# Mixed attention and expert layer, one core: expert weights in 2 MB pieces with 16 KB rows to a partition

## The chip, the core and the metric

One core of one Trainium2 chip runs the whole program. The metric is the device time of one execution in microseconds (us); less is better. All data is in the chip's main memory (HBM) at the start, and the result is written back there.

## The reference, cut to what matters

One transformer-like layer on 256 latent tokens of 1024 channels, with 256 context tokens. A first part (attention, a gated linear attention and an output projection) makes `x_next`. The second part is a mixture of 32 experts, and it is the part that the change is about:

```python
h2 = rms_norm(x_next, norm2) * (1 + sc2) + sh2
logits = h2 @ w_router + b_router               # top 4 of 32 experts for each token
...
gu   = xb @ w1[e] + b1[e]                       # w1: 1024 x 2048 fp32 for each expert, 8 MB
gate = minimum(gu[:, :1024], 7.0)
up   = clip(gu[:, 1024:], -7.0, 7.0)
act  = gate * sigmoid(1.702 * gate) * (up + 1)
y    = act @ w2[e] + b2[e]                      # w2: 1024 x 1024 fp32 for each expert, 4 MB
...
x = x_next + gt2 * weighted_sum_of_the_four(y)
```

Everything is fp32. The weights of all experts are 32 x 12 MB = 402.65 million bytes, and the kernel reads each of them once.

## The kernel before

The kernel is written with a framework that places the tiles, sets the waits and chooses the order of the instructions on each engine by a schedule of its own; the order on an engine is then fixed. All transfers between HBM and the on-chip memory (SBUF) are issued by SyncE (SP in the profile), one after another: an issue that waits for its buffer holds up all issues behind it. The bytes of a transfer are spread over 16 DMA engines, 8 of the 128 partitions to each.

**The first part** (up to about 325 us) loads its weights by `raw_load` (L115) into a pool `wp` of four rotating buffers of 8 KB to a partition. `split` (L120) makes of each fp32 piece a high and a low part (ScalarE L123, VectorE L124) in a second pool `spl` of two buffers, also of 8 KB. The last weights that go this way are the four pieces of `w_out` (L871). Their output is `xn`, from which `hsc`, `h2h` and `h2l` are made (L894 to L897): the normalised tokens, and their high and low parts. Router, top 4 and positions follow (L901 to L928), then a gather by matmul (`gather`, L1000) that puts the tokens of an expert into columns of `xs`, at most 63 of them; the rest, if any expert has more, goes to a fallback loop (L1180) that does not run here.

**The expert part.** For expert e, `layer1` (L1027) multiplies `xs` with the eight blocks of 128 rows of w1 (k = 0 to 7), each block in one 1 MB piece with a row of 8 KB to a partition. `scale1` (L1034) copies the two PSUM banks to `gu` on ScalarE (L1038); `fold` (L1041) transposes and adds the two halves by matmul (L1044), adds the bias `b1T` and does the activation (L1047 to L1055) into `x.a`. `layer2` (L1057) multiplies `x.a` with w2, four 1 MB pieces of two blocks of 128 rows, two rows of 4 KB to a partition. `scatter` (L1072) adds the result to the output banks. The order is layer 1 of expert e, then layer 2 of expert e-1; the list `order` (L949) has the loads in the same order: 8 pieces of w1, then 4 of w2, 384 pieces in all.

**The buffers of the pieces** (`load_next`, L958) are taken in turn from 15 places of 1 MB: four of a pool `raw2`, the two halves of `xhl`, the four buffers of `wp`, the two halves of `xhh`, the two of `spl` and one of `mp`. `raw2` and `xhl` come free early. Those of `wp` and `spl` come free when the pieces of `w_out` have been split and used, one after another; `xhh` (the memory of `yh`, `yl`) after the last matmul of `w_out` (L797); that of `mp` after the router. `weights` (L987) hands a piece to the matmuls.

Other names in the rows: `ml`, `wb`, `wo` are weights of the first part, `wb` and `wo` with rows of 2 KB; `c` is the bank of layer 2, `g` that of layer 1, `t` that of fold, `ga` or `y` that of gather, `y` also the output.

Of the kernel before, what the change touches and what calls it, by code (L numbers as in the profile page):

```python
# [73 lines left out]
def layer(tc, t, dbg=None):  # L74
# [10 lines left out]
    dram = es.enter_context(tc.tile_pool(name="dram", bufs=1, space=DRAM))  # L85
    wp = es.enter_context(tc.tile_pool(name="wp", bufs=2))
    spl = es.enter_context(tc.tile_pool(name="spl", bufs=2))

# [3 lines left out]
    hhf = hh.rearrange("p k n -> p (k n)")  # L92
    NRAW, NMORE, NSPL = 4, 1, 2

# [20 lines left out]
    def raw_load(src, name):  # L115
        r = wp.tile(list(src.shape), F32, tag="raw", name=name, bufs=NRAW)
        queue.append(sp.dma_start(r, src))
        return r

    def split(r, name, after=None):  # L120
        hl_ = spl.tile([P, 2] + list(r.shape[1:]), F32R, tag="w", name=name + "s", bufs=NSPL)
        h, l = hl_[:, 0], hl_[:, 1]
        a = act.activation(h, r, AF.Copy)  # L123
        b = dve.tensor_sub(l, r, h.bitcast(F32))  # L124
        if after:
            behind(a, after[0])
            behind(b, after[1])
        return h, l
# [95 lines left out]
    load_mod(1)  # L224
    load_pa(1)
    queue.append(sp.dma_start(wlr, win[:, 2304:2336].rearrange("(k p) n -> p k n", p=P)))
    pbch = kchunks(win, 512, 512, "pb")
    for a, b in zip(queue, queue[1:]):
        behind(b, a)
    front = queue[-1]  # L230

# [246 lines left out]
    clr = bx.tile([P, 33 * P], F32R, tag="lsg", name="clr")  # L478
    clu = wp.tile([P, 33 * P], U8, tag="raw", name="clu", bufs=NRAW)
    sp.dma_start(clu, t["cl"])  # L480
# [347 lines left out]
    sp.dma_start(rt[0:16], mrow[:, D:3 * D].rearrange("o (k p) -> (o k) p", p=P))  # L828
    sp.dma_start(rt[16:24], t["norm2"].rearrange("o (k p) -> (o k) p", p=P))
    wr = mx.tile([P, KB, NE], F32, name="wr")  # L830
    sp.dma_start(wr, t["w_router"][0].rearrange("(k p) n -> p k n", p=P))
    brb = keep.tile([P, NE], F32, name="brb")
    sp.dma_start(brb, t["b_router"].to_broadcast([P, NE]))
    b1T = keep.tile([P, NE, 16], F32, name="b1T")
    bt = mx.tile([P, 4, P], F32, name="bt")
    sp.dma_start(bt, t["b_exp_in"][0].rearrange("e (b p) -> (e b) p", p=P).rearrange("(j p) n -> p j n", p=P))
    b1p = glb("b1p")
    for j in range(4):
        pe.transpose(b1p[:, j * P:(j + 1) * P], bt[:, j], ident)
    dve.tensor_copy(b1T, b1p.rearrange("p (e b) -> p e b", b=16))  # L840
    rtp = glb("rtp")
# [28 lines left out]
    for n in range(2):  # L870
# [76 lines left out]


    order = []  # L949
    for e in range(NE + 1):  # L950
        if e < NE:
            order += [(e, k) for k in range(KB)]
        if e:
            order += [(e - 1, KB + q) for q in range(KB // 2)]
    loads, ready = [0], {}
    NROT = 4 + 2 * NRAW + NSPL + NMORE

    def load_next():  # L958
        n = loads[0]
        loads[0] += 1  # L960
        if n >= len(order):
            return
        e, k = order[n]
        m = n % NROT
        if m < NRAW:
            r = raw2.tile([P, 2048], F32, tag="raw", name=f"x{e}_{k}", bufs=NRAW)
        elif m < 2 + NRAW:
            m -= NRAW
            r = xhl[:, m * 2048:(m + 1) * 2048]
        elif m < 2 + 2 * NRAW:  # L970
            r = wp.tile([P, 2048], F32, tag="raw", name=f"x{e}_{k}", bufs=NRAW)
        elif m < 4 + 2 * NRAW:
            m -= 2 + 2 * NRAW
            r = xhh[:, m * 2048:(m + 1) * 2048]
        elif m < 4 + 2 * NRAW + NSPL:
            r = spl.tile([P, 2048], F32, tag="w", name=f"x{e}_{k}", bufs=NSPL)
        else:
            r = mp.tile([P, 2048], F32, tag="raw", name=f"x{e}_{k}", bufs=NMORE)
        if k < KB:
            sp.dma_start(r, w1[e][k * P:(k + 1) * P])  # L980
        else:
            q = k - KB
            sp.dma_start(r.rearrange("p (k n) -> p k n", k=2),
                         w2[e][q * 2 * P:(q + 1) * 2 * P].rearrange("(k p) n -> p k n", p=P))
        ready[e, k] = r

    def weights(e, k):  # L987
        while (e, k) not in ready:
# [38 lines left out]
    def layer1(x, xs, k):  # L1027
        w = weights(x.e, k)
# [28 lines left out]
    def layer2(x):  # L1057
        b = bank(gp, "c", f"c{x.e}")
        for q in range(KB // 2):
            w = weights(x.e, KB + q).rearrange("p (k n) -> p k n", k=2)  # L1060
            for kk in range(2):
                k = 2 * q + kk
                for n in range(2):
                    pe.matmul(b[n * CAP:(n + 1) * CAP], x.a[:, k], w[:, kk, n * 512:(n + 1) * 512],  # L1064
                              start=k == 0, stop=k == KB - 1)
        oh = mp.tile([P, 512], F32R, tag="oh", name=f"oh{x.e}", bufs=2)
# [113 lines left out]
    with tc.If(most > LIM):  # L1180
# [18 lines left out]
        with tc.For_i(0, NE, 1) as e:  # L1199
# [80 lines left out]
```

## Time and profile before

| | us |
|---|---|
| runs shown | 1317.69, 1317.51, 1295.82 (median 1317.51) |
| the profiled execution | 1295.6 |
| its span, first to last instruction | 1293.8 |

TensorE (PE) is busy 1202.9 us of the span, VectorE (DVE) 383.5, ScalarE (ACT) 254.9, GpSimd (POOL) 45.3. In the chain that ended last PE has 55% and DMA 39%. Busy PE is not PE at its peak: matmuls are pipelined and their ends are modelled. "PEld" is the weight load of PE. A row of the timeline has the start in us, the duration, the engine, the line, what is written from what, the number of instructions merged, and in brackets the idle time before it with what ended it.

### The profile page before, as it was taken

What the parts mean: (1) busy time and instruction counts of PE and PEld (TensorE: products, weight loads), DVE (VectorE), ACT (ScalarE), POOL (GpSimd) and SP (SyncE); (2) the same over time, 40 slices, a digit from 0 to 9 for tenths busy, and PEclk for the clock granted to TensorE, in tenths of its full rate; (3) what the DMA queues carried; (4) which work ended last, traced back from release to release, by engine and by line L of the source; (5) the groups of instructions that cost most, each with busy time, mean ns of one, the idle gap of its engine ahead of it and who ended that gap; (6) DMA issues with size and microseconds to landing.
All of it is one profiled execution on the core that took longest, in us unless ns stands there. A gap on an engine that the chain in (4) does not pass through costs nothing.

```text
span 1293.8 us, 14788 instructions
## 1 busy us (share of the span) xinstructions
PE 1202.9 (93%) x6050; PEld 564.5 (44%) x6050; DVE 383.5 (30%) x830; ACT 254.9 (20%) x445; POOL 45.3 (3%) x52
## 2 busy tenths in 40 slices
PE   6999999999899999999989998999899899988886
PEld 4667868767443344333323332333333333322222
DVE  4556766457411131311111111211121111111113
ACT  3453433434111111111111111111111111111110
POOL 1201000002200000000000000000000000000000
PEclk9999999999899999999999999999999999999998
DMA  9856111895999999999999999999999999999995
GB/s 344 295 174 229 67 48 54 320 385 183 352 414 418 417 417 417 417 418 417 417 417 417 416 417 417 416 417 419 417 417 417 418 419 417 416 416 417 417 417 213
DMA packets 98707, 463.80 MB, mean 358 GB/s; under 512 B 10270, under 2 KB 12418, under 8 KB 63818
## 3 DMA queue, kind: packets, MB, share of 16 engines
q1 hardware_dynamic: 98636, 462.82, 89.4%
q8 instruction: 49, 0.80, 0.3%
q14 instruction: 22, 0.18, 0.0%
HBM read 461.73 MB, written 1.06 MB: 358 GB/s over the span
## 4 chain that ended last, share of the span: by engine, by line
PE 55%; DMA 39%; DVE 2%; issue 1%; ACT 1%; POOL 1%; SPq 0%; POOLq 0%; DVEq 0%; ACTq 0%
DMA x<-in_w_exp_in 32%; PE g L1031 14%; PE c L1064 12%; DMA x<-in_w_exp_out 5%; PE t L1044 4%; PE pg L289 3%; PE br L797 2%; PE pa L289 2%; DMA xhh<-in_w_exp_out 2%; PE pc L289 1%; PE pb L289 1%; PE ml L395 1%; PE o L697 1%; PE e L535 1%; PE a L560 1%
## 5 line engine op out<-in xcount | busy, mean ns | idle before, releaser
L1031 PE MATMUL g<-x,xs 128*64 128x512 f32 x1536 | 365.5, 600 | 35.9 <-DMA x<-in_w_exp_in 35.9
L1031 PEld LDWEIGHTS g<-x,xs 128*64 128x64 f32 x1536 | 100.7, 136 | 261.9 <-issue 153.7
L1047 DVE TENSOR_TENSOR o<-t,b1T 128x512 f32<-128x512 f32 x64 | 44.3, 692 | 543.5 <-PE t L1044 543.5
L1064 PE MATMUL c<-x,a 128*64 128x512 f32 x720 | 172.5, 603 | 0.6 <-DMA x<-in_w_exp_out 0.6
L1038 ACT ACTIVATE gu<-g,ws 128x512 f32<-128x512 f32 x64 | 43.6, 687 | 456.2 <-PE g L1031 455.2
L1044 PEld LDWEIGHTS t<-cf,gu 128*128 128x128 f32 x512 | 62.0, 191 | 51.2 <-ACT sg L1052 22.7
L1064 PEld LDWEIGHTS c<-x,a 128*64 128x64 f32 x720 | 44.7, 136 | 68.9 <-issue 56.3
L1044 PE MATMUL t<-cf,gu 128*128 128x128 f32 x512 | 74.0, 288 | 0.0
L1031 PE MATMUL g<-xhl,xs 128*64 128x512 f32 x256 | 63.0, 600 | 5.4 <-DMA xhl<-in_w_exp_in 5.4
L1031 PE MATMUL g<-xhh,xs 128*64 128x512 f32 x256 | 62.1, 599 | 5.4 <-DMA xhh<-in_w_exp_in 5.4
L1052 ACT ACTIVATE sg<-o 128x256 f32<-128x256 f32 x64 | 26.6, 416 | 158.2 <-DVE o L1050 158.2
L1069 DVE SCALAR_TENSOR_TENSOR ol<-c,ws,oh 128x512 fp32r<-128x512 f32 x32 | 24.0, 749 | 82.8 <-ACT oh L1068 82.8
L1068 ACT ACTIVATE oh<-c,ws 128x512 fp32r<-128x512 f32 x32 | 22.0, 688 | 109.8 <-PE c L1064 109.8
L1064 PE MATMUL c<-xhl,a 128*64 128x512 f32 x160 | 39.6, 605 | 0.6 <-DMA xhl<-in_w_exp_out 0.6
L1007 DVE COPY xs<-ga 128x252 f32<-128x252 f32 x28 | 11.8, 421 | 87.8 <-PE ga L1003 87.8
L1031 PEld LDWEIGHTS g<-xhh,xs 128*64 128x64 f32 x256 | 17.3, 136 | 43.8 <-issue 27.1
L1031 PEld LDWEIGHTS g<-xhl,xs 128*64 128x64 f32 x256 | 17.5, 136 | 43.2 <-issue 27.2
L1003 PEld LDWEIGHTS ga<-G,h2h 128*128 128x128 f32 x112 | 16.7, 188 | 44.9 <-issue 44.9
L1064 PE MATMUL c<-xhh,a 128*64 128x512 f32 x144 | 34.6, 604 | 0.0
L1077 PE MATMUL y<-oh,st 64*128 64x512 f32 x128 | 23.7, 445 | 10.8 <-ACT oh L1068 8.7
L1054 DVE TENSOR_TENSOR sg<-sg,o 128x256 f32<-128x256 f32 x64 | 27.2, 425 | 17.9 <-ACT sg L1052 17.9
L1003 PE MATMUL ga<-G,h2h 128*128 128x256 f32 x112 | 28.2, 333 | 0.0
(583 smaller groups left out, 1336.7 us busy)
## 6 DMA issues: line engine op xcount, KB each, us to landing
x<-in_w_exp_in SPq DMA_DIRECT2D x192, 1024.0 KB
x<-in_w_exp_out SPq DMA_DIRECT2D x90, 1024.0 KB
xhl<-in_w_exp_in SPq DMA_DIRECT2D x32, 1024.0 KB
xhh<-in_w_exp_in SPq DMA_DIRECT2D x32, 1024.0 KB
xhl<-in_w_exp_out SPq DMA_DIRECT2D x20, 1024.0 KB
xhh<-in_w_exp_out SPq DMA_DIRECT2D x18, 1024.0 KB
ml<-in_w_mod SPq DMA_DIRECT2D x16, 1024.0 KB
wm<-in_w_mod SPq DMA_DIRECT2D x16, 512.0 KB
```

The lines of the kernel that those rows point to most:

```text
L289: m_ = pe.matmul(b[:, 0:m], a[:, k, i * P:(i + 1) * P], w[:, kk, 0:m], start=k == 0 and x == 0, stop=k == KB - 1 and x == 2)
L797: pe.matmul(b, a[:, k, i * P:(i + 1) * P], w[:, kk], start=first and p + kk + x == 0, stop=last and p == 1 and kk == 1 and x == 2)
L1003: pe.matmul(b[:, 0:256], src[:, i, k * P:(k + 1) * P], G[:, i, :, 0], start=hf + i == 0, stop=hf + i == 2)
L1031: pe.matmul(x.gu[h][u * CAP:(u + 1) * CAP], xs[:, x.e % GS, k], w[:, u * D + h * 512:u * D + h * 512 + 512], start=k == 0, stop=k == KB - 1)
L1038: act.activation(gu, x.gu[h], AF.Copy, scale=x.r)
L1044: pe.matmul(b[:, j * P:(j + 1) * P], x.gs[h][:, j * P:(j + 1) * P], foldm, start=True, stop=True)
L1047: dve.tensor_tensor(o, b.rearrange("p (b u s) -> p b u s", b=4, u=2), bias.unsqueeze(3).to_broadcast([P, 4, 2, CAP]), op=ALU.add)
L1052: act.activation(s, g, AF.Sigmoid, scale=1.702)
L1054: dve.tensor_mul(s, s, g)
L1064: pe.matmul(b[n * CAP:(n + 1) * CAP], x.a[:, k], w[:, kk, n * 512:(n + 1) * 512], start=k == 0, stop=k == KB - 1)
L1069: dve.scalar_tensor_tensor(ol, b, x.w, oh.bitcast(F32), op0=ALU.mult, op1=ALU.subtract)
L1077: pe.matmul(ys[i][n], x.st[r, i * P:(i + 1) * P], x.o[q][r], start=False, stop=x.e == NE - 1 and q == 1, skip_group_check=True)
```

## The change

Expert weights are loaded in pieces of 2 MB in which a partition has 16 KB of neighbouring rows: partition p of a w1 piece has rows 2p and 2p+1 of a block of 256, of a w2 piece rows 4p to 4p+3 of a block of 512. The tokens and the hidden units are permuted to match (`h2h`, `h2l`, `gu`, `b1T`, `shc`), so that the same products are summed. The 15 places of 1 MB become 7 of 2 MB, taken in turn, and one of 1 MB used once; one piece of expert 1 and the very last one are loaded in two halves of 1 MB. For this `wp` and `spl` are no longer pools with rotating buffers: `wp` is two fixed tiles of 16 KB to a partition, used in the first part as four places in turn by `raw_tile`, and `spl` is one tile with two halves. As a place is now given in the order of the program text, the calls of `load_pa(1)`, `wlr` and `pb` are moved down behind the code that reads the place before; the order of the queue is the same.

```diff
-    NRAW, NMORE, NSPL = 4, 1, 2
+    NRAW, NSPL = 4, 2
+    wpt = [wp.tile([P, 4096], F32, name=f"wpt{j}") for j in range(2)]
+    spt = spl.tile([P, 4096], F32R, tag="spt", name="spt")
+    ring = [0, 0]
+
+    def raw_tile(shape, name=None, dt=F32):
+        n = ring[0] = ring[0] + 1
+        r = wpt[(n - 1) // 2 % 2][:, (n - 1) % 2 * 2048:(n - 1) % 2 * 2048 + 2048]
...
+    def split_tile(shape):
+        n = ring[1] = ring[1] + 1
+        r = spt[:, (n - 1) % 2 * 2048:(n - 1) % 2 * 2048 + 2048]
...
     def raw_load(src, name):
-        r = wp.tile(list(src.shape), F32, tag="raw", name=name, bufs=NRAW)
+        r = raw_tile(list(src.shape)[1:])
...
-        hl_ = spl.tile([P, 2] + list(r.shape[1:]), F32R, tag="w", name=name + "s", bufs=NSPL)
+        hl_ = split_tile(list(r.shape[1:]))
...
-    raw2 = es.enter_context(tc.tile_pool(name="raw2", bufs=NRAW, side="right"))
+    raw2 = es.enter_context(tc.tile_pool(name="raw2", bufs=2, side="right"))
...
+    rts = mx.tile([4, 2 * P], F32, name="rts")
+    sp.dma_start(rts, mrow[:, D:2 * D].rearrange("o (q c) -> (o q) c", q=4))
...
-    bt = mx.tile([P, 4, P], F32, name="bt")
-    sp.dma_start(bt, t["b_exp_in"][0].rearrange("e (b p) -> (e b) p", p=P).rearrange("(j p) n -> p j n", p=P))
+    bt = mx.tile([P, 512], F32, name="bt")
+    sp.dma_start(bt, t["b_exp_in"][0].rearrange("e (b n) -> (e b) n", n=512))
...
-    pool.tensor_copy(shc[:, :, 0], rtT[:, 0:8])
+    for kk in range(2):
+        pe.transpose(rtp[:, 32 + 4 * kk:36 + 4 * kk], rts.rearrange("q (c k) -> q k c", k=2)[:, kk], ident[0:4, 0:4])
+    dve.tensor_copy(shc[:, :, 0].rearrange("p (q k) -> p k q", k=2), rtp[:, 32:40].rearrange("p (k q) -> p k q", k=2))
...
-            act.activation(h2h[:, i, sl], h2, AF.Copy)
-            (dve if n else pool).tensor_sub(h2l[:, i, sl], h2, h2h[:, i, sl].bitcast(F32))
+            by = lambda a: a.rearrange("p (q c k) -> p q k c", k=2, c=P)
+            to = lambda a: a[:, i, sl].rearrange("p (q k c) -> p q k c", k=2, c=P)
+            act.activation(to(h2h), by(h2), AF.Copy)
+            (dve if n else pool).tensor_sub(to(h2l), by(h2), to(h2h).bitcast(F32))
...
-            order += [(e, k) for k in range(KB)]
+            order += [(e, 0, q, None) for q in range(4)]
+            if e == 1:
+                order[-1:] = [(e, 0, 3, 0), (e, 0, 3, 1)]
         if e:
-            order += [(e - 1, KB + q) for q in range(KB // 2)]
-    loads, ready = [0], {}
-    NROT = 4 + 2 * NRAW + NSPL + NMORE
+            order += [(e - 1, 1, q, None) for q in range(2)]
+    order[-1:] = [(NE - 1, 1, 1, 0), (NE - 1, 1, 1, 1)]
+    loads, ready = [0, 0], {}
+    whole = [raw2.tile([P, 4096], F32, tag="raw", name=f"xr{j}", bufs=2) for j in range(2)]
+    whole += [xhl] + wpt + [xhh, spl.tile([P, 4096], F32, tag="spt", name="xsp")]
+    small = mp.tile([P, 2048], F32, tag="raw", name="xs")
...
+            r = whole[loads[1] % len(whole)]
...
+            w = w1[e][q * 2 * P:(q + 1) * 2 * P].rearrange("(p k) n -> p k n", k=2)
+            w = w.rearrange("p k n -> p (k n)") if h is None else w[:, h]
...
+            w = w2[e][q * 4 * P:(q + 1) * 4 * P].rearrange("(p k) n -> p k n", k=4)
...
-            act.activation(gu, x.gu[h], AF.Copy, scale=x.r)
+            act.activation(gu.rearrange("p (j c) -> p j c", j=4), x.gu[h].rearrange("p (c j) -> p j c", j=4), AF.Copy, scale=x.r)
```

Left out of the diff: the moved calls, `b1T` written by a permuted copy, `layer2` over eight blocks instead of four pairs, and the same permutations in the fallback loop.

## Rows read from the trace of the kernel before

**Rows 1.** The page: busy time, granted clock, GB/s in 40 slices, packets.

```profile
PE 1202.9 (93%) x6050; PEld 564.5 (44%) x6050; DVE 383.5 (30%) x830; ACT 254.9 (20%) x445; POOL 45.3 (3%) x52
...
PEclk9999999999899999999999999999999999999998
...
GB/s 344 295 174 229 67 48 54 320 385 183 352 414 418 417 417 417 417 418 417 417 417 417 416 417 417 416 417 419 417 417 417 418 419 417 416 416 417 417 417 213
DMA packets 98707, 463.80 MB, mean 358 GB/s; under 512 B 10270, under 2 KB 12418, under 8 KB 63818
```

**Rows 2.** Busy time by stretch, the expert part in two stages.

```profile
core 0: us, PE busy (x) PEld busy (x) DVE busy (x) ACT busy (x) POOL busy (x), PEclk, DMA share, GB/s
400.00:640.00 240.00, 237.81 (x1174) 96.29 (x1176) 54.47 (x132) 34.41 (x68) 1.84 (x3) 1.00 1.02 417
640.00:1260.00 620.00, 565.52 (x2684) 203.40 (x2684) 107.92 (x259) 71.45 (x136) 1.84 (x3) 1.00 1.02 417
```

**Rows 3.** Waits from 640 to 1290 us: total us, times, longest.

```profile
PEld g L1031 <- DMA x<-in_w_exp_in: 103.0, 85, 2.3
...
PE g L1031 <- DMA x<-in_w_exp_in: 35.9, 65, 1.4
```

**Rows 4.** Timeline of PE: scatter matmuls of experts in the first stage.

```profile
528.03 0.73 PE L1077 MATMUL y<-oh,st 64*128 64x512 f32 x4
...
637.27 0.74 PE L1077 MATMUL y<-oh,st 64*128 64x512 f32 x4
```

**Rows 5.** Timeline of PE: first matmuls on pieces that PE waited for.

```profile
1198.64 1.94 PE L1031 MATMUL g<-x,xs 128*64 128x512 f32 x8 [0.58 <-DMA x<-in_w_exp_in]
...
1218.75 1.94 PE L1031 MATMUL g<-x,xs 128*64 128x512 f32 x8 [0.38 <-DMA x<-in_w_exp_in]
...
1228.71 1.94 PE L1031 MATMUL g<-x,xs 128*64 128x512 f32 x8 [0.55 <-DMA x<-in_w_exp_in]
```

**Rows 6.** Stretches with one kind of rows: 8 KB, 4 KB, 2 KB.

```profile
356.00:364.00 8.00, 8.00 (x41) 3.98 (x41) 2.04 (x5) 2.39 (x3) 0.00 (x0) 1.00 1.02 425
1262.00:1271.00 9.00, 8.38 (x43) 3.19 (x43) 4.07 (x10) 1.02 (x3) 0.00 (x0) 1.00 1.02 409
265.00:268.00 3.00, 3.00 (x15) 2.49 (x14) 1.23 (x1) 0.28 (x1) 0.00 (x0) 1.00 0.99 383
```

**Rows 7.** Timeline of SP: issues of expert pieces before and at the start.

```profile
299.27 0.36 SPq L980 DMA_DIRECT2D x<-in_w_exp_in  x1
...
306.36 0.35 SPq L980 DMA_DIRECT2D x<-in_w_exp_in  x1
...
314.10 0.33 SPq L980 DMA_DIRECT2D x<-in_w_exp_in  x1
...
322.11 1.00 SPq L980 DMA_DIRECT2D x<-in_w_exp_in  x2
...
340.50 0.35 SPq L980 DMA_DIRECT2D x<-in_w_exp_in  x1
```

**Rows 8.** Stretches at the start of the expert part.

```profile
320.00:324.00 4.00, 3.45 (x20) 2.99 (x21) 2.59 (x4) 0.24 (x1) 1.00 (x1) 1.00 0.15 39
340.00:344.00 4.00, 4.00 (x29) 2.67 (x27) 0.58 (x2) 1.04 (x3) 1.64 (x3) 1.00 0.72 229
344.00:348.00 4.00, 4.00 (x20) 1.29 (x18) 0.00 (x0) 0.00 (x0) 2.02 (x2) 1.00 0.78 261
```

**Rows 9.** Groups by line: the copies that become strided (L896, L897 of 280:345).

```profile
L1038 ACT ACTIVATE gu<-g,ws 128x512 f32<-128x512 f32 x64 | 43.6, 687 | 456.2 <-PE g L1031 455.2
...
L897 POOL TENSOR_TENSOR h2l<-hsc,h2h 128x512 fp32r<-128x512 f32 x2 | 2.9, 1466 | 0.0
...
L896 ACT ACTIVATE h2h<-hsc 128x512 fp32r<-128x512 f32 x4 | 2.5, 624 | 1.4 <-POOL hsc L895 1.4
```

**Rows 10.** Timeline of PE: the last piece.

```profile
1279.79 1.94 PE L1064 MATMUL c<-x,a 128*64 128x512 f32 x8 [0.57 <-DMA x<-in_w_exp_out]
```

More of the change, by code (lines that the diff above doesn't have):

```diff
@@ L85, in layer @@
     dram = es.enter_context(tc.tile_pool(name="dram", bufs=1, space=DRAM))
-    wp = es.enter_context(tc.tile_pool(name="wp", bufs=2))
-    spl = es.enter_context(tc.tile_pool(name="spl", bufs=2))
+    wp = es.enter_context(tc.tile_pool(name="wp", bufs=1))
+    spl = es.enter_context(tc.tile_pool(name="spl", bufs=1))
     px = es.enter_context(tc.tile_pool(name="px", bufs=1))
@@ L92, in layer @@
     hhf = hh.rearrange("p k n -> p (k n)")
-    NRAW, NMORE, NSPL = 4, 1, 2
+    NRAW, NSPL = 4, 2
[5 more added lines that the diff above has]
+        r = wpt[(n - 1) // 2 % 2][:, (n - 1) % 2 * 2048:(n - 1) % 2 * 2048 + 2048]
+        if dt is not F32:
+            return r.bitcast(dt)[:, 0:shape[0]]
+        r = r[:, 0:int(np.prod(shape))]
+        if len(shape) == 2:
+            return r.rearrange("p (a b) -> p a b", a=shape[0])
+        return r.rearrange("p (a b c) -> p a b c", a=shape[0], b=shape[1])
+    def split_tile(shape):
+        n = ring[1] = ring[1] + 1
+        r = spt[:, (n - 1) % 2 * 2048:(n - 1) % 2 * 2048 + 2048]
+        r = r.rearrange("p (x n) -> p x n", x=2)[:, :, 0:shape[0] * shape[1]]
+        return r.rearrange("p x (a b) -> p x a b", a=shape[0])
     class low:
@@ L211, in load_mod @@
             else:
-                r = wp.tile([P, 2, 2, 512], F32, tag="raw", name=f"wm{g}{q}", bufs=NRAW)
+                r = raw_tile([2, 2, 512])
             for kk in range(2):
@@ L224, in layer @@
     load_mod(1)
[L225 to L230, printed above, removed]
     smp = glb("smp")
@@ L357, in layer @@
         pass
+    load_pa(1)
+    queue.append(sp.dma_start(wlr, win[:, 2304:2336].rearrange("(k p) n -> p k n", p=P)))
     modulate(0)
@@ L361, in layer @@
     next(pag)
+    pbch = kchunks(win, 512, 512, "pb")
+    for a, b in zip(queue, queue[1:]):
+        behind(b, a)
+    front = queue[-1]
     for p in (2, 3):
@@ L478, in layer @@
     clr = bx.tile([P, 33 * P], F32R, tag="lsg", name="clr")
-    clu = wp.tile([P, 33 * P], U8, tag="raw", name="clu", bufs=NRAW)
+    clu = raw_tile([33 * P], dt=U8)
     sp.dma_start(clu, t["cl"])
@@ L958, in load_next @@
+    whole = [raw2.tile([P, 4096], F32, tag="raw", name=f"xr{j}", bufs=2) for j in range(2)]
+    whole += [xhl] + wpt + [xhh, spl.tile([P, 4096], F32, tag="spt", name="xsp")]
+    small = mp.tile([P, 2048], F32, tag="raw", name="xs")
     def load_next():
-        n = loads[0]
+        if loads[0] >= len(order):
+            return
+        e, l, q, h = order[loads[0]]
         loads[0] += 1
[L961 to L976, printed above, removed]
-        else:
-            r = mp.tile([P, 2048], F32, tag="raw", name=f"x{e}_{k}", bufs=NMORE)
@@ L979, in load_next @@
-        if k < KB:
-            sp.dma_start(r, w1[e][k * P:(k + 1) * P])
-        else:
[L982 to L988, printed above, removed]
+        if (e, l, q, h) == (1, 0, 3, 0):
+            r = small
+        else:
+            r = whole[loads[1] % len(whole)]
+            loads[1] += 1
+            if h is not None:
+                r = r[:, 0:2048]
@@ new lines, in load_next @@
+        if l == 0:
+            w = w1[e][q * 2 * P:(q + 1) * 2 * P].rearrange("(p k) n -> p k n", k=2)
+            w = w.rearrange("p k n -> p (k n)") if h is None else w[:, h]
+            parts = range(2) if h is None else (h,)
+        else:
+            w = w2[e][q * 4 * P:(q + 1) * 4 * P].rearrange("(p k) n -> p k n", k=4)
+            w = w.rearrange("p k n -> p (k n)") if h is None else w[:, 2 * h:2 * h + 2].rearrange("p k n -> p (k n)")
+            parts = range(4) if h is None else (2 * h, 2 * h + 1)
@@ L989, in weights @@
+        sp.dma_start(r, w)
+        n = D if l else 2 * D
+        for x, k in enumerate(parts):
+            ready[e, l, len(range(4 if l else 2)) * q + k] = r[:, x * n:(x + 1) * n]
+    def weights(e, l, k):
+        while (e, l, k) not in ready:
             load_next()
-        load_next()
-        return ready.pop((e, k))
+        if k % (4 if l else 2) == 0:
+            load_next()
+        return ready.pop((e, l, k))
     def group_hot(g):
@@ L1027, in layer1 @@
     def layer1(x, xs, k):
-        w = weights(x.e, k)
+        w = weights(x.e, 0, k)
         for h in range(2):
@@ L1058, in layer2 @@
         b = bank(gp, "c", f"c{x.e}")
[L1059 to L1065, printed above, removed]
+        for k in range(KB):
+            w = weights(x.e, 1, k)
+            for n in range(2):
+                pe.matmul(b[n * CAP:(n + 1) * CAP], x.a[:, k], w[:, n * 512:(n + 1) * 512],
+                          start=k == 0, stop=k == KB - 1)
         oh = mp.tile([P, 512], F32R, tag="oh", name=f"oh{x.e}", bufs=2)
@@ L1190, in layer @@
             h2 = fp.tile([P, D], F32, tag="fh2", name=f"fh2{i}")
-            dve.tensor_add(h2, h2h[:, i].bitcast(F32), h2l[:, i].bitcast(F32))
+            nat = lambda a: a[:, i].bitcast(F32).rearrange("p (q k c) -> p q k c", k=2, c=P)
+            dve.tensor_add(h2.rearrange("p (q c k) -> p q k c", k=2, c=P), nat(h2h), nat(h2l))
             dve.scalar_tensor_tensor(h2, h2, r2[:, i:i + 1], sh, op0=ALU.mult, op1=ALU.add)
@@ L1208, in layer @@
                     for q in range(2):
-                        w = wp.tile([P, 4, 512], F32, tag="raw", name=f"fw{g}{q}", bufs=NRAW)
+                        w = raw_tile([4, 512])
                         c0 = GC[2 * hf + g]
@@ L1217, in layer @@
                         for k in range(KB):
-                            pe.matmul(bs[g][:, 0:256], ws[2 * g + k // 4][:, k % 4, b4 * P:(b4 + 1) * P], hT[:, k],
+                            pe.matmul(bs[g][:, 0:256], ws[2 * g + k // 4][:, k % 4].rearrange("p (c j) -> p j c", j=4)[:, b4], hT[:, k],
                                       start=k == 0, stop=k == KB - 1)
```

8 lines of the change are left out of this document (4 added, 4 removed).

## The prediction

> **What bounds the kernel now.** I read the page first, then busy time by stretch, the waits, and two timelines. The page shows PE busy for 93% of the span at full clock, which looks like a kernel bound by PE, but from slice 12 on the DMA line stands at 414 to 419 GB/s and never leaves it [rows 1]. By stretch the expert part has two stages [rows 2]. From 400 to 640 us PE is busy 237.8 of 240 us; from 640 to 1260 it is busy 565.5 of 620. DMA moves 417 GB/s in both. The waits of the second stage are for pieces of w_exp_in, 103.0 us by the weight loads of PE and 35.9 by its matmuls [rows 3]. So PE starts with 15 pieces in hand, works the lead off until about 640 us, and from then on takes each piece as it lands.
>
> Two periods say the same. PE alone needs (637.27 - 528.03) / 4 = 27.31 us for an expert, between two scatters four experts apart [rows 4]. DMA needs 12.58 MB / 417 GB/s = 30.17 us. In the timeline of PE, pieces of w1 land 2.49 us apart, (1228.71 - 1218.75) / 4; between 1198.64 and 1218.75 lie four pieces of w1 and four of w2, so a w2 piece takes (20.11 - 4 x 2.49) / 4 = 2.54 us [rows 5]; 8 x 2.49 + 4 x 2.54 = 30.1. The end is set by the DMA stream: its last piece lands at 1279.8 us [rows 10], and 14 us of work follow. A gain must come from the rate of the stream or from its start.
>
> **The change part by part.**
>
> *The rows.* This is the main term. A w1 piece has 8 rows of 8 KB for each DMA engine, a w2 piece 16 of 4 KB: 8 x 8 + 4 x 16 = 128 rows for each engine and expert, 65,536 of the 98,707 packets in all [rows 1]. With 16 KB it is 6 x 8 = 48, so 80 fewer, with the same bytes. What is a row worth? By the landings, 8 more rows in a megabyte cost 2.5375 - 2.49 = 0.047 us: 5.9 ns for a row [rows 5]. By the mean rates of stretches with one kind of rows, 425, 409 and 383 GB/s make 2.467, 2.564 and 2.738 us for 1 MB, so 12 ns for a row from 8 to 4 KB and 11 from 4 to 2 KB [rows 6] (the last stretch is not wholly of 2 KB rows). The landings are set by the slowest engine, and they are what PE waits for; the mean rate counts faster engines too. So I take 7 ns, near the landings: 80 x 7 ns = 0.56 us for an expert, x 32 = 18 us. The ends: 5.9 ns gives 15 us, 12 ns gives 31. No row of 16 KB is in the trace, so nothing at all is possible too; that is a rival. That 194 transfers do the work of 384 I price at nothing up to a row each, 190 x 12 ns = 2.3 us, since they queue behind one another.
>
> The Trainium skill ("DMA: Bandwidth & Descriptors", section "Where 436 GB/s comes from") gives a ceiling of 435.2 GB/s at the ports of the on-chip memory. By it an expert can't take less than 28.9 us and the change can't win more than 40 us; the trace stays below it.
>
> *Does PE become the bound?* At 29.6 us for an expert PE still has 2.3 us to spare against its 27.31 [rows 4]. Its lead lasts longer, to about 750 us, and costs nothing.
>
> *The copies that become strided.* ScalarE's `gu` copy takes 687 ns, 64 times [rows 9]; read with a step of four it takes between that and twice that. At worst the fold of an expert comes 0.7 us later, inside the 2.3 us that PE has left. In the first part ScalarE's `h2h` (624 ns) and GpSimd's `h2l` (1466 ns) read every second element [rows 9]; those of the second half stand on the way to the first expert matmul. Twice as long is up to 2.6 us there, but the stream feels it only through the first buffers that come back; I take 0.3.
>
> *The buffers at the start.* Before, pieces go out as each 1 MB place is given up by `w_out`: 299.27, 306.36, 314.10, two at 322.11 [rows 7]. Now the fourth 2 MB piece wants `wpt0`, whose halves hold the last two pieces of `w_out`, so it can't go before 322; and if SP's order has it ahead of the piece for `wpt1` (free at 306), that waits too. What moves behind 322 is 1 to 3 MB, at 2.49 us each 2.5 to 7.5 us of load time. The stream had idle time to take it up: DMA was at 0.15 in 320 to 324 and at 0.72 and 0.78 in 340 to 348 [rows 8], which is 1.1 + 0.9 us in the latter and about 1.5 after 322 in the former, 3.5 in all. So the start costs 0 to 4 us; I take 1.7, as I can't see which piece SP's schedule puts first. Behind the waiting issue stand only pieces for `xhh` and `spl`, free after 322 themselves. With the strided copies: 2 us.
>
> *The rest.* The fixed ring has the same four places in the same turn as the pool before, so the first part should keep its times; the moved calls don't change the queue's order. `rts`, two small transposes and a copy are off the path, and `b_exp_in` goes in 128 rows instead of 512. The last megabyte is again a piece of its own, so the tail after it stays. The 2 MB w1 piece costs PE 1.75 us more after landing than a 1 MB one, but w2 follows it and hides that.
>
> **Sum.** 1295.6 - 18 + 2 = 1279.6, say 1280 us, 1.2% less. The profiled execution, 1295.6, agrees with the lowest of the runs shown (1295.82); the median, 1317.51, lies 22 us higher, on two runs that agree with each other. If the kernel after falls into that group its time is some 1302, which the range includes.
>
> **The rivals.**
>
> *Rows of 8 KB are already long enough* (0.15). Then only w2 wins, the difference of 0.047 us (landings) to 0.097 (rates) on 4 MB: 0.19 to 0.39 us for an expert, 6 to 12 us in all, and 1286 to 1292; I write 1288. For it: 8 KB rows run at 425 GB/s, above every slice of the page [rows 6, 1]. Against it: the price of a row is about the same from 2 to 4 and from 4 to 8 KB, and doesn't fade. The Trainium skill has a rule of this kind in the same page, section "Why small descriptors are slow": a packet costs three beats of 32 bytes on top of its own. With the 311 ns of an 8 KB row (259 beats) that is an estimate of 3.6 ns a row and 9 us in all, 1288. By that rule the trace should show w2 1.2% behind w1; it shows 1.9% by landings and 4% by rates.
>
> *The full price of the mean rate* (0.2). 12 ns a row: 31 us, 1266.6, 2.2% less. For it: two steps of the row size give the same price. Against it: the slowest engine shows half of it, and PE waits for that one.
>
> *Nothing is won* (0.1). A 16 KB row may be cut into pieces of 8 KB or less on the way, or another limit stands at 425 GB/s. Then 1297.6. The packet count would tell.
>
> *The pieces come back too late* (0.1), the case that ends above the time before. Place: the first experts, 340 to 440 us, where PE is the slower one. A 2 MB place is free only when all its rows are used. Between the last w1 place and the first of w2 PE does two folds, the transposes of `start` and the four blocks of a w2 piece, about 6.5 us, against 4.9 us that DMA needs for a piece; if all seven places are full the stream stands 1.6 us in each of the first three experts, 5 us, with the 4 of the worst start 9. It decides when a row is worth less than 9 us / (80 x 32) = 3.5 ns; with no gain at all it is 1304.6, slower than before by 0.7%. For it: idle DMA is there already at 340 to 348 [rows 8]. Against it: from 360 on DMA never idles with 15 MB of places, and there are still 14.
>
> **How the numbers follow.** The forecast (a gain of 15 to 24 us, 1272 to 1283) has 0.45, the rivals 0.15, 0.2, 0.1 and 0.1 as written. The likeliest is 1280. The range goes from 1264, the full price with a free start and a little for fewer transfers, to 1303, the late pieces, which also takes in the forecast in the upper group of runs. A measurement of this kernel can tell about 2% from no change, which is 26 us. Faster by more than that needs most of the full price: its 0.2 for the greater part and a little of the forecast's fast side and of the spread of runs, 0.26. Slower by 2% needs a loss that I don't see in the rows, 0.05. Within 2%: 0.69.
>
> **What would show it right or wrong.** Some 58,000 packets instead of 98,707. DMA between 423 and 427 GB/s in the stretch of waits, against 417; 419 or less would mean the second or fourth case, 430 and more the full price. Pieces 4.90 to 4.95 us apart for w1 and for w2 alike. An expert in 29.6 us; PE still waiting for w_exp_in in the last third. At the start an issue to `wpt0` at about 322 us, and DMA without a gap from there to 347. The forecast is wrong if the rate stays at 417, if the period falls to 27.3 with PE without waits, or if the first expert matmul moves by over 5 us from 338.5.

## The result, and the profile after

The changed kernel takes 1281.59 us in the median of four runs (1280.06 to 1305.86); the kernel before, now with four runs, 1307.91 (1295.82 to 1317.69). Single executions of most of these kernels, the traced one of long rows for w2 alone below among them, come out some 20 to 25 us higher, with a lower granted clock in the first part and the same DMA rate from 400 us on (428 GB/s in one of the changed kernel, against 427); without those the ratio is 0.9874 [0.9851, 0.9896], a gain of 1.3%, clear of noise but under 2%. The profiled executions are 1280.06 and 1295.6 us, the spans 1278.2 and 1293.8: 15.6 us less. The forecast was 1280.

The page of the kernel after: busy times, GB/s in 40 slices, packets.

```profile
PE 1184.2 (93%) x6052; PEld 578.7 (45%) x6052; DVE 378.9 (30%) x831; ACT 254.8 (20%) x445; POOL 44.8 (4%) x51
...
GB/s 345 300 180 218 65 64 34 302 401 182 286 410 428 428 427 430 427 427 427 429 426 429 427 427 426 428 428 427 428 428 427 427 429 428 426 427 428 426 429 182
DMA packets 54584, 463.77 MB, mean 363 GB/s; under 512 B 7234, under 2 KB 8874, under 8 KB 27634
```

Against [rows 1] the DMA line stands still from slice 13 on (the first slice is 1; the last is the end), but at 426 to 430 GB/s instead of 416 to 419. In slice 11, where the expert part has just begun, it is lower than before: 286 against 352, and 410 against 414 in slice 12. So there is a faster stream and a poorer start, and both can be read from stretches. Busy time by stretch of the kernel after:

```profile
core 0: us, PE busy (x) PEld busy (x) DVE busy (x) ACT busy (x) POOL busy (x), PEclk, DMA share, GB/s
300.00:400.00 100.00, 92.89 (x450) 50.00 (x450) 38.07 (x78) 22.48 (x40) 13.85 (x15) 0.95 0.80 320
400.00:640.00 240.00, 229.19 (x1137) 94.32 (x1133) 51.58 (x128) 32.98 (x65) 1.23 (x2) 1.00 1.01 428
400.00:1240.00 840.00, 782.50 (x3850) 311.72 (x3846) 158.68 (x391) 105.57 (x204) 3.69 (x6) 1.00 1.01 427
```

The same view of the kernel before, for two stretches that [rows 2] does not have:

```profile
300.00:400.00 100.00, 92.93 (x455) 49.76 (x453) 37.35 (x77) 22.88 (x41) 15.02 (x16) 0.97 0.85 337
400.00:1240.00 840.00, 787.33 (x3786) 295.35 (x3788) 161.64 (x390) 105.17 (x203) 3.68 (x6) 1.00 1.02 417
```

From 300 to 400 us 33.7 MB came in before, 32.0 after: 1.7 MB less, which at 427 GB/s is 4.0 us. (It is a net figure: in part of this stretch the longer rows are already at work.) From 400 us to the landing of the last w1 piece the faster stream saves 859 x (1 - 417/427) = 20 us. That landing is read from the first matmul on the piece: after it stands at 1242.61 (the line is shown under the tail, further down), before here (timeline of PE):

```profile
1259.45 1.94 PE L1031 MATMUL g<-x,xs 128*64 128x512 f32 x8 [0.55 <-DMA x<-in_w_exp_in]
```

It moved 16.8 us earlier, about the 20 less 4.0, and from it to the end it is 35.6 us instead of 34.4: 1.2 given back. That leaves the 15.6 us of the spans.

First matmuls on pieces that PE waited for, timeline of PE after. A line has the start, the duration, the engine, the operation, the number of merged instructions, and in brackets the idle time before:

```profile
1143.43 3.65 PE L1059 MATMUL g<-xsp,xs 128*64 128x512 f32 x16 [0.40 <-DMA xsp<-in_w_exp_in]
...
1148.33 3.65 PE L1059 MATMUL g<-xr,xs 128*64 128x512 f32 x16 [1.25 <-DMA xr<-in_w_exp_in]
...
1153.23 3.65 PE L1059 MATMUL g<-xr,xs 128*64 128x512 f32 x16 [1.24 <-DMA xr<-in_w_exp_in]
```

A piece of 2 MB lands each 4.90 us, where two of 1 MB took 4.98 [rows 5]. PE is still the one that waits, but much less. The waits from 640 to 1290 us:

```profile
PEld g L1059 <- DMA xr<-in_w_exp_in: 11.5, 8, 2.1
PEld g L1059 <- DMA xsp<-in_w_exp_in: 8.4, 4, 2.7
PEld g L1059 <- DMA xhh<-in_w_exp_in: 8.2, 5, 3.2
PEld g L1059 <- DMA wpt<-in_w_exp_in: 8.0, 8, 1.5
...
PEld g L1059 <- DMA xhl<-in_w_exp_in: 4.3, 2, 2.1
```

The weight loads of layer 1 wait 40.4 us in these five rows, against 103.0 in the largest row before [rows 3]. The first matmul that waits for a piece of w1 comes at 886 us, where it was 650 before (timelines of PE, before and after):

```profile
649.95 1.94 PE L1031 MATMUL g<-x,xs 128*64 128x512 f32 x8 [0.55 <-DMA x<-in_w_exp_in]
```

```profile
886.10 3.65 PE L1059 MATMUL g<-wpt,xs 128*64 128x512 f32 x16 [0.49 <-DMA wpt<-in_w_exp_in]
```

### The profile page after: what moved, and what is told of

The parts are those of the page before. It is cut to its first block, busy times and chain, and to the rows that moved or that the text cites. A ratio compares the mean times of both kernels' runs of the same rounds, so it can differ in the third digit from the quotient of the medians.

```text
span 1278.2 us, 14416 instructions
## 1 busy us (share of the span) xinstructions
PE 1184.2 (93%) x6052; PEld 578.7 (45%) x6052; DVE 378.9 (30%) x831; ACT 254.8 (20%) x445; POOL 44.8 (4%) x51
## 2 busy tenths in 40 slices
DMA packets 54584, 463.77 MB, mean 363 GB/s; under 512 B 7234, under 2 KB 8874, under 8 KB 27634
## 4 chain that ended last, share of the span: by engine, by line
PE 70%; DMA 21%; DVE 4%; ACT 2%; issue 1%; POOL 1%; SPq 0%; POOLq 0%; DVEq 0%; ACTq 0%
PE g L1059 26%; PE c L1090 13%; DMA xhh<-in_w_exp_in 10%; DMA xhl<-in_w_exp_in 5%; PE t L1072 4%; PE pg L302 3%; DMA xr<-in_w_exp_in 2%; DMA xsp<-in_w_exp_out 2%; DMA wpt<-in_w_exp_in 2%; PE ga L1031 2%; PE br L816 2%; PE y L1103 2%; PE pa L302 2%; PE ml L414 1%; PE pc L302 1%
## 5 line engine op out<-in xcount | busy, mean ns | idle before, releaser
L1059 PE MATMUL g<-wpt,xs 128*64 128x512 f32 x608 | 140.7, 596 | 2.2 <-DMA wpt<-in_w_exp_in 1.9
L1059 PE MATMUL g<-xr,xs 128*64 128x512 f32 x552 | 126.1, 599 | 5.0 <-DMA xr<-in_w_exp_in 4.9
L1072 PE MATMUL t<-cf,gu 128*128 128x128 f32 x512 | 73.7, 287 | 17.5 <-DVE o L1075 17.5
L1072 PEld LDWEIGHTS t<-cf,gu 128*128 128x128 f32 x512 | 62.1, 191 | 56.5 <-issue 32.1
L1059 PEld LDWEIGHTS g<-wpt,xs 128*64 128x64 f32 x608 | 42.7, 137 | 85.7 <-issue 76.9
L1090 PE MATMUL c<-xr,a 128*64 128x512 f32 x336 | 76.6, 598 | 0.0
L143 DVE TENSOR_TENSOR spt<-wpt,spt 128x1024 fp32r<-128x1024 f32 (+1 forms) x52 | 62.5, 1202 | 46.3 <-ACT spt L142 46.2
L1059 PEld LDWEIGHTS g<-xr,xs 128*64 128x64 f32 x552 | 38.1, 137 | 80.9 <-issue 68.2
L1059 PE MATMUL g<-xsp,xs 128*64 128x512 f32 x288 | 67.3, 596 | 4.8 <-DMA xsp<-in_w_exp_in 4.8
L142 ACT ACTIVATE spt<-wpt 128x1024 fp32r<-128x1024 f32 (+1 forms) x52 | 53.2, 1024 | 78.1 <-PE pg L302 22.9
L1090 PE MATMUL c<-wpt,a 128*64 128x512 f32 x264 | 60.3, 598 | 0.4 <-DMA wpt<-in_w_exp_out 0.2
L302 PE MATMUL pg<-spt,hh 128*128 128x512 f32 x128 | 41.8, 402 | 0.0
```

What stands on the lines that cost most here:

```text
L302: m_ = pe.matmul(b[:, 0:m], a[:, k, i * P:(i + 1) * P], w[:, kk, 0:m], start=k == 0 and x == 0, stop=k == KB - 1 and x == 2)
L1072: pe.matmul(b[:, j * P:(j + 1) * P], x.gs[h][:, j * P:(j + 1) * P], foldm, start=True, stop=True)
L1090: pe.matmul(b[n * CAP:(n + 1) * CAP], x.a[:, k], w[:, n * 512:(n + 1) * 512], start=k == 0, stop=k == KB - 1)
```

## The experiments

Each runs against the kernel before, and those of a group on the same chip; the ratios are all to the kernel before. The question behind them: is it the length of the rows that wins, or the size of the transfers, and what do the coarser places take back?

### The old rows in 2 MB transfers

A partition takes its two (w1) or four (w2) rows from places 128 rows apart, as before; transfers, places and order stay as in the changed kernel. The kernel leaves out the right pairing of rows with tokens and hidden units, and so does each of the next two for the matrix with the old rows.

```diff
-            w = w1[e][q * 2 * P:(q + 1) * 2 * P].rearrange("(p k) n -> p k n", k=2)
+            w = w1[e][q * 2 * P:(q + 1) * 2 * P].rearrange("(k p) n -> p k n", k=2)
...
-            w = w2[e][q * 4 * P:(q + 1) * 4 * P].rearrange("(p k) n -> p k n", k=4)
+            w = w2[e][q * 4 * P:(q + 1) * 4 * P].rearrange("(k p) n -> p k n", k=4)
...
-        sp.dma_start(r, w)
+        sp.dma_start(r.rearrange("p (k n) -> p k n", k=w.shape[1]), w)
```

> The changed kernel with its 2 MB transfers, places, order and copies, but with the rows of before inside each transfer (two rows of 8 KB for w1, four of 4 KB for w2 to a partition; the rows meet other tokens and hidden units, so the product left out is the right pairing). Theory A, the rows: 128 rows again for each engine and expert, so DMA falls from 427 to 417 GB/s in 400 to 1240 us and the time rises by 20 to 23 us to some 1302. Theory B, the size and number of transfers: it stays at 425 to 428 GB/s and at 1280 to 1284 us.

Measured: 1303.08 us, ratio 1.0051 [1.0034, 1.0067]. The packets on its page:

```profile
DMA packets 95288, 463.77 MB, mean 356 GB/s; under 512 B 7234, under 2 KB 8874, under 8 KB 60402
```

And its stretch from 400 to 1240 us:

```profile
400.00:1240.00 840.00, 764.67 (x3748) 302.46 (x3744) 153.81 (x379) 102.93 (x199) 3.69 (x6) 1.00 1.02 417
```

The rate is that of the kernel before, 417, with half as many transfers. So the size of the transfer gives nothing; without the long rows the change is a loss of 0.5%, some 6.6 us. Between this kernel and the changed one only the rows differ: 1.0051 - 0.9874 = 0.0177, some 23 us. Its landings give the price by kind of row (timeline of PE; w2 with 4 KB rows, then w1 with 8 KB rows):

```profile
967.62 3.65 PE L1090 MATMUL c<-xhl,a 128*64 128x512 f32 x16 [0.37 <-DMA xhl<-in_w_exp_out]
...
972.71 3.65 PE L1090 MATMUL c<-wpt,a 128*64 128x512 f32 x16 [0.35 <-DMA wpt<-in_w_exp_out]
...
1166.13 3.65 PE L1059 MATMUL g<-xsp,xs 128*64 128x512 f32 x16 [0.99 <-DMA xsp<-in_w_exp_in]
...
1171.11 3.65 PE L1059 MATMUL g<-xr,xs 128*64 128x512 f32 x16 [1.32 <-DMA xr<-in_w_exp_in]
```

2 MB take 5.09 us in rows of 4 KB, 4.98 in rows of 8 KB and 4.90 in rows of 16 KB. For a DMA engine these are 32, 16 and 8 rows: 0.11/16 = 7 ns a row in the first step, 0.08/8 = 10 ns in the second. These are single readings: the next landing in the same trace is 5.01 behind, not 4.98, and 0.02 us makes 2.5 ns in the second step. So the landings cannot tell the two steps apart.

### Long rows for w1 alone, and for w2 alone

The same edit, for the other matrix alone in each.

> Rows of 16 KB for w1 alone, four rows of 4 KB for w2 (the pairing of w2's rows with hidden units is not the reference's). 96 rows for each engine and expert. Theory A with one price for a row (9.6 ns from 128 rows at 417 and 48 at 428 GB/s): 29.86 us for an expert, 421 GB/s, about 1293 us. Theory C, rows of 8 KB are long enough: nothing is kept of the gain, 417 to 418 GB/s and about 1301 us.

> Rows of 16 KB for w2 alone, two rows of 8 KB for w1 (the pairing of w1's rows with tokens' channels is not the reference's). 80 rows for each engine and expert. Theory A: 29.71 us for an expert, 423 to 424 GB/s, about 1289 us. Theory C: the whole gain is kept, 427 GB/s and about 1281 us.

Measured with w1 alone: 1293.92 us, ratio 0.9984 [0.9969, 0.9999]. With w2 alone: 1289.99 us, ratio 0.9946 [0.9929, 0.9962]. The stretch from 400 to 1240 us, first w1 alone:

```profile
400.00:1240.00 840.00, 772.13 (x3794) 307.23 (x3792) 157.96 (x390) 104.91 (x203) 3.70 (x6) 1.00 1.01 421
```

Then w2 alone:

```profile
400.00:1240.00 840.00, 778.11 (x3821) 309.35 (x3819) 155.50 (x382) 103.39 (x200) 3.70 (x6) 1.00 1.01 423
```

With 128, 96, 80 and 48 rows for each engine and expert the rate is 417, 421, 423 and 427 GB/s. An expert's 12.58 MB then take 30.17, 29.88, 29.74 and 29.46 us. With long rows for w1 alone 32 rows and 0.29 us go, for w2 alone 48 rows and 0.43 us: 9 ns a row in both, between the two readings of the forecast. w1 wins 0.0067 for its 32 rows, w2 0.0105 for its 48, and 0.0067 + 0.0105 = 0.0172 is about the whole 0.0177. The rival by which rows of 8 KB are already long enough falls: by it w1 alone would have stayed where all old rows are. The packets in the traces say it too: from 400 to 1240 us one lasts 163 ns in mean with 4 KB, 314 with 8 KB and 616 with 16 KB, so one packet less is worth 12 to 13 ns of an engine in both steps. Why the stream gains 9 of them is not shown.

The Trainium skill ("DMA: Bandwidth & Descriptors", section "Why small descriptors are slow") has three beats on top of each packet, estimated at 3.6 ns by the 311 ns of an 8 KB row. The trace shows 9 ns between rows of 4 and 16 KB, so the measurement decides: the rule names the right kind of cost and less than half of its size here.

### The same rows cut in two by columns

Each 2 MB piece goes as two transfers of all 128 partitions, each with half a row of 16 KB: 8 KB rows, 96 for an engine and expert, as with w1 alone, but twice as many transfers, and the places are returned by halves.

```diff
-        sp.dma_start(r, w)
+        for c in range(0, r.shape[1], 2048):
+            sp.dma_start(r[:, c:c + 2048], w[:, c:c + 2048])
```

> The changed kernel with every 2 MB piece issued as two transfers of all 128 partitions, each with one half of the 16 KB row: rows of 8 KB everywhere, 96 for each engine and expert, as in the run with 16 KB for w1 alone, but in 384 transfers instead of 194. If only rows cost: 421 GB/s in 400 to 1240 us, as there, and at most its 1294 us; half places can be loaded again one by one, so up to 4 us less, 1290 to 1294. If a transfer costs something too: below 420 GB/s, and the difference to 421 is its price (1 GB/s is 0.07 us for an expert, 12 ns for each of the 6 transfers more on an engine). If cutting by partitions was slow because there are more transfers: 218 GB/s and over 1850 us.

Measured: 1289.5 us, ratio 0.9937 [0.9917, 0.9956]. Stretches of this kernel:

```profile
300.00:400.00 100.00, 94.10 (x454) 51.48 (x454) 37.61 (x78) 22.84 (x41) 14.68 (x15) 0.93 0.85 329
400.00:640.00 240.00, 237.81 (x1174) 96.21 (x1172) 54.46 (x132) 34.40 (x68) 1.84 (x3) 1.00 1.01 421
400.00:1240.00 840.00, 791.76 (x3812) 297.88 (x3808) 162.38 (x391) 105.85 (x204) 3.69 (x6) 1.00 1.01 421
```

421 GB/s with 96 rows, once with 194 transfers and once with 384 (421.13 and 421.07 by the packets of the two traces, which makes under 0.2 us in all): a transfer that queues behind others costs nothing that shows; only rows do. The rows read here are the long ones of the changed kernel, so it is not which rows a partition takes that sets the rate, but into how many packets they are cut. And with the same rate this kernel is faster than the one with w1 alone, by 0.0047 or 6 us in the ratios, by 4.0 us between the two profiled spans. It has 329 GB/s in 300 to 400 us, the other, whose stretch follows, 313 (1.6 MB, 3.8 us):

```profile
300.00:400.00 100.00, 92.85 (x452) 50.56 (x452) 38.16 (x78) 23.07 (x41) 13.91 (x15) 0.95 0.80 313
```

That is what whole 2 MB places cost more at the start than places returned by halves. In 400 to 640 us PE is busy 237.8 us as before [rows 2], with whole pieces 229.2; that is taken up further down.

### Each piece as two transfers of 64 partitions

```diff
-        sp.dma_start(r, w)
+        for c in range(2):
+            sp.dma_start(r[c * 64:c * 64 + 64], w[c * 64:c * 64 + 64])
```

> The changed kernel with every expert piece issued as two transfers, partitions 0 to 63 and 64 to 127: the same rows of 16 KB, 48 for each engine and expert, in twice as many transfers of half the size. Theory A: 427 to 428 GB/s and 1279 to 1284 us (a transfer of its own costs up to 12 ns on an engine, 2 us in all). Theory B: 420 GB/s or less and over 1293 us.

Measured: 1919.35 us in the median of four (1887.16 to 2005.06); the ratio of the two shortest is 1.4593 [1.4548, 1.4638]. Both expectations were far off. The stretch from 400 to 1240 us:

```profile
400.00:1240.00 840.00, 537.39 (x1980) 202.47 (x1981) 81.27 (x201) 54.99 (x107) 2.45 (x4) 0.81 1.01 218
```

DMA has a share of 1.01, so its engines are busy all the time, and move half as much, 218 GB/s instead of 427. Number and length of the rows are as in the changed kernel; what differs is that a transfer fills only half of the partitions. This one could not tell anything about the price of a transfer, which is why the cut by columns was made.

By the Trainium skill ("SBUF — State Buffer", section "Door 1: The DMA port swizzle") partitions 0 to 63 reach only half of the 16 ports of the on-chip memory, 64 to 127 the other half, and its limit for half of them is 218 GB/s; the trace agrees with 218.

### The start and the tail in 1 MB halves

Three attempts to get back what the coarse places cost, with the changed kernel once more on the same chip:

> The changed kernel again, as a measure for the three beside it: 1280 to 1282 us, 0.987 of before, in 300 to 400 us 320 GB/s.

The start: the pieces whose 2 MB place comes free by halves, or is wanted early, go in two, and `wpt1`, free at 306 us, comes ahead of `wpt0`.

```diff
-            if e == 1:
-                order[-1:] = [(e, 0, 3, 0), (e, 0, 3, 1)]
+            cut = {0: (3,), 1: (0, 3), 2: (0,)}.get(e, ())
+            order[-4:] = [(e, 0, q, h) for q in range(4) for h in ((0, 1) if q in cut else (None,))]
...
-    whole += [xhl] + wpt + [xhh, spl.tile([P, 4096], F32, tag="spt", name="xsp")]
+    whole += [xhl] + wpt[::-1] + [xhh, spl.tile([P, 4096], F32, tag="spt", name="xsp")]
```

> The changed kernel with the loads of the start cut into halves of 1 MB with rows of 8 KB: the last w1 piece of expert 0 and the first of expert 1 (into wpt1, then wpt0, half by half as w_out gives them up), w2 of expert 0 and the first w1 piece of expert 2 (half by half as the first places come back). Theory, the late places cost 4 us at the start: DMA moves 335 GB/s or more in 300 to 400 us instead of 320, and the time falls by 3 to 4 us against the changed kernel, to about 1277. Rival, the end is set by PE after the last w1 piece so that the stream's start no longer counts, or SP's order undoes it: 1280 to 1282 us.

The tail: the last w1 piece goes in two halves.

```diff
+            if e == NE - 1:
+                order[-1:] = [(e, 0, 3, 0), (e, 0, 3, 1)]
...
```

> The changed kernel with the last w1 piece of expert 31 cut into halves of 1 MB, so that PE can start its first block of rows 2.4 us before the second lands. Theory, PE works without a wait from the landing of that piece to the end: the time falls by about 1.7 us, the time of one block of layer 1, to 1279. Rival, the last w2 piece sets the end as before the change: no difference, 1280 to 1282 us.

Both at once:

> The halves of the start and of the tail together: the two gains add, 4.5 to 6 us less than the changed kernel, 1275 to 1277 us, if both theories hold; 1280 if the end hides the start.

Measured, as ratios to the kernel before: the changed kernel again 0.9866 [0.9848, 0.9884]; start in halves 0.985 [0.9838, 0.9862] and 1277.87 us, the best of all; tail in halves 0.9871 [0.9854, 0.9888]; both 0.9861 [0.9843, 0.9879].

The start in halves leads by some 2 us, where 3 to 4 were expected, and its interval overlaps that of the changed kernel, so the gain itself is not shown. Its stretch:

```profile
300.00:400.00 100.00, 93.23 (x453) 50.38 (x452) 37.48 (x78) 22.91 (x41) 14.63 (x15) 0.95 0.84 323
```

Its first issues on SP (start, time to the end of the last merged one):

```profile
299.14 0.36 SPq L1017 DMA_DIRECT2D wpt<-in_w_exp_in  x1
306.22 16.20 SPq L1017 DMA_DIRECT2D wpt<-in_w_exp_in  x3
```

The first issue is back at 299.14, as before [rows 7], but the mean is 323 GB/s and not the 335 that was expected, against 320 without the halves. The tail in halves gains nothing. PE no longer waits for the last half of w1, and then waits for w2 instead (timeline of PE, tail in halves):

```profile
1255.37 3.65 PE L1094 MATMUL c<-xr,a 128*64 128x512 f32 x16 [0.98 <-DMA xr<-in_w_exp_out]
```

Both together bring no more than the start alone, and whether the tail costs anything there stays below what these runs can tell.

## Why the prediction was right

**What bounds the kernel: right.** The stream sets the end before and after. Between the changed kernel and the one with the old rows only the stream's rate differs, 427 and 417, and the 23 us between them are what that rate makes of 32 experts: 32 x (30.17 - 29.46).

**The rows: the mechanism was right, the size too small.** "So I take 7 ns, near the landings: 80 x 7 ns = 0.56 us for an expert, x 32 = 18 us." The runs show 9 ns and some 23 us. The step that failed is the choice between two readings of the price: the landings [rows 5] gave 5.9 ns, the mean rates of short stretches [rows 6] 12, and 7 was set near the landings. The landings were read too coarsely for that: in the runs they give 7 ns again from 4 to 8 KB, where the rates of whole stages give 9 (128 rows at 417 GB/s, 96 rows of 8 KB at 421). And 48 of the 80 rows that go lie between 8 and 16 KB, where no row of the kernel before could show a price; it is 9 ns there too. The landings after the change sum up to nearly the same: four pieces of w1 at 4.98 - 4.90 and two of w2 at 5.09 - 4.90 are 0.70 us for an expert, 22 us in all. The bounds of 15 and 31 held it.

**Transfers at nothing: right.** It was shown by the cut by columns.

**The start: beyond the bounds.** "So the start costs 0 to 4 us; I take 1.7" and, with the strided copies, 2. The 4.0 us by bytes above would be the upper bound, but the longer rows have already paid part of them back, and the 18 us of the forecast count that gain once more. The price by itself stands in the run with the old rows, which wins nothing by rows:

```profile
300.00:400.00 100.00, 93.28 (x453) 51.66 (x453) 39.16 (x80) 23.06 (x41) 13.86 (x15) 0.95 0.81 311
```

311 GB/s against 337 before are 2.6 MB, 6.2 us at 417 GB/s; with the 1.2 us of the tail it is 7.4, within the bounds of the 6.6 us [4.4, 8.7] that this kernel loses. The reasons can be read in the issues of SP after the change:

```profile
305.57 16.88 SPq L1009 DMA_DIRECT2D wpt<-in_w_exp_in  x2
324.74 0.33 SPq L1009 DMA_DIRECT2D xhh<-in_w_exp_in  x1
...
341.92 0.35 SPq L1009 DMA_DIRECT2D xr<-in_w_exp_in  x1
349.29 0.35 SPq L1009 DMA_DIRECT2D xr<-in_w_exp_out  x1
```

The first is the one that was named: one piece of 2 MB leaves at 305.57 and the next only at 322.1, where before 3 MB had been issued by 314.10 and two more followed at 322.11 [rows 7]. The second is the rival *The pieces come back too late*: after 341.92 nothing is issued for 7.4 us, until PE has used the second block of the first place and both of the second (timeline of PE):

```profile
343.87 5.37 PE L1059 MATMUL g<-xr,xs 128*64 128x512 f32 x24
```

Before, a place of half the size was free at 344.42. The stretches after the change show it:

```profile
300.00:320.00 20.00, 19.26 (x88) 14.82 (x88) 15.79 (x17) 10.39 (x15) 6.45 (x4) 1.00 0.37 132
320.00:324.00 4.00, 3.49 (x21) 2.77 (x20) 2.55 (x5) 0.00 (x0) 0.06 (x1) 1.00 0.29 61
...
340.00:344.00 4.00, 4.00 (x27) 2.55 (x25) 0.42 (x1) 0.41 (x2) 0.00 (x0) 0.92 0.96 272
344.00:348.00 4.00, 4.00 (x20) 1.36 (x22) 0.16 (x1) 0.63 (x2) 3.57 (x4) 1.00 0.55 213
348.00:352.00 4.00, 4.00 (x18) 1.22 (x16) 0.42 (x1) 0.00 (x0) 0.10 (x1) 1.00 0.43 102
352.00:356.00 4.00, 4.00 (x20) 1.29 (x18) 0.00 (x0) 0.00 (x0) 0.00 (x0) 1.00 1.00 426
```

And the kernel before, where [rows 8] has no row:

```profile
300.00:320.00 20.00, 19.32 (x89) 14.90 (x87) 15.08 (x17) 10.56 (x16) 6.74 (x5) 1.00 0.51 190
...
348.00:352.00 4.00, 4.00 (x18) 1.22 (x16) 0.42 (x1) 0.00 (x0) 0.00 (x0) 1.00 1.02 401
352.00:356.00 4.00, 4.00 (x19) 1.18 (x15) 0.00 (x0) 0.69 (x1) 0.00 (x0) 1.00 0.85 338
```

Up to 324 us 2.9 MB came in after and 4.0 before, from 340 to 356 us 4.1 and 4.9: 1.1 and 0.9 MB, of which 324 to 340 us gave 0.2 back. The forecast counted the idle time of 340 to 348 as room to catch up; instead the late return of the second place made more of it, and its sign "DMA without a gap from there to 347" did not come (share 0.55 from 344 to 348). The strided copies cost little: `gu` takes 687 ns as before, ScalarE's `h2h` 665 instead of 624 ns, GpSimd's `h2l` 1892 instead of 1466 [rows 9], and the first expert matmul starts at 339.32 instead of 338.52; what these 0.8 us cost the stream is not shown apart.

**The tail: wrong by a little.** "The last megabyte is again a piece of its own, so the tail after it stays." The last megabyte was no longer what the end waits for. Timeline of PE after, from the last w1 piece:

```profile
1242.61 3.65 PE L1059 MATMUL g<-xhh,xs 128*64 128x512 f32 x16 [2.36 <-DMA xhh<-in_w_exp_in]
1246.19 1.16 PE L1072 MATMUL t<-cf,gu 128*128 128x128 f32 x8
1248.23 1.13 PE L1072 MATMUL t<-cf,gu 128*128 128x128 f32 x8 [0.88 <-DVE o L1075]
...
1263.82 1.89 PE L1090 MATMUL c<-wpt,a 128*64 128x512 f32 x8
```

Behind the last w1 piece PE never waits for DMA again; before, it waited at 1279.79 [rows 10]. The way to the end is now PE's own work on that piece, two blocks of 128 rows where there was one, and the folds: 1.2 us more, by the profile alone.

**PE's margin: held, but thinner than written.** "PE still has 2.3 us to spare against its 27.31 [rows 4]." PE's own period grew. Scatters of the kernel after, in the stage where PE has work in hand:

```profile
534.04 0.73 PE L1103 MATMUL y<-oh,st 64*128 64x512 f32 x4
...
647.14 0.73 PE L1103 MATMUL y<-oh,st 64*128 64x512 f32 x4
```

They are (647.14 - 534.04) / 4 = 28.28 us for an expert, against 27.31 [rows 4], with 29.46 of the stream: 1.2 us to spare. Before, a piece of w2 stood between the two transposes of a fold (L1044, L1064, L1044); now the second group of L1072 follows the first and waits 0.9 us for DVE, as at 1248.23. With pieces cut by columns, PE is as busy in 400 to 640 us as before. The permutation is the same there, so it is an effect of the whole pieces on the order that the framework chooses. It cost no time here, since PE has the lead; the lead went out at 886 us, not at 750 as forecast, which fits 1.2 us an expert using it up slower than 2.3.

**The sum.** 1295.6 - 18 + 2 = 1279.6 was forecast. By the terms as the runs measure them, each by itself, it is 1295.6 - 22.7 + 6.2 + 1.2 = 1280.3, against 1280.06 in the profiled execution. The total was much nearer than its terms: the gain was 5 us too small, the losses 5 us too small, and the two cancel. That the number came out so closely is luck.

The rivals: with 8 KB rows long enough, w1 alone would have had no gain; at the full price of the mean rate, the stream should have stood at 430 GB/s and more; nothing won is excluded by 427. The late pieces exist: with the late start and the tail they cost 6.6 us, where their rival had 9, and with no gain by rows the kernel is slower than before, by 0.5% where that rival wrote 0.7% and 1304.6 us (the range, meant to take it in, ended at 1303). They did not decide, since a row is worth 9 ns and not under 3.5.

## What to carry to other kernels

In a stream that sets the end, count rows for each DMA engine, not transfers, since the bytes stay the same. Price a row by the rates of long stretches with two row lengths (9 ns here, still between 8 and 16 KB); landings read to 0.02 us and stretches of a few us gave 6 and 12. Longer rows and larger places are two edits: cut a piece by columns and the places return sooner but the rows halve; so keep the long rows for the stream, and go by halves only for the few pieces whose places come free late. When a sum comes out, check its terms; here two errors of 5 us hid each other. A run without the gain, here the one with the old rows, gives the loss by itself.

## What the runs showed of the hardware that was not expected

Two transfers of 64 partitions, one behind the other, ran at 218 GB/s, half of what one of 128 reaches, with the DMA engines shown busy throughout.

The price of a row does not fade with its length: by the rates it is 9 ns from 4 to 8 KB (417 GB/s with 128 rows, 421 with 96 of 8 KB) and 9 from 8 to 16 (427 with 48).

Each transfer brings 16 small packets of its own. The packets of the kernel cut by columns:

```profile
DMA packets 81947, 463.81 MB, mean 360 GB/s; under 512 B 10274, under 2 KB 11914, under 8 KB 30674
```

From 194 transfers to 384 the packets under 512 B go from 7,234 to 10,274, 16 for each; before, also with 384, they were 10,270 [rows 1]. That is why the packets came out at 54,584 and not at the forecast's 58,000: 80 x 16 x 32 fewer rows leave 57,747, and 190 x 16 fewer small packets 54,707. They cost no rate that shows.
